# A two-layer hybrid decoder trunk on one core: attention in pairs of heads, one values block for eight heads, the decay table in the queries' place

## The chip, the core and the metric

The kernel runs on one core of one Trainium2 chip. The metric is the device time of one execution in microseconds (us). Three runs of the kernel before gave 844.59, 845.5 and 845.59 us; the median is 845.5 us. The profile comes from a further execution that took 844.61 us, of which the span from the first to the last recorded instruction is 842.8 us.

## The reference, cut to what matters

256 tokens of width 1024 pass two layers, all in float32. A layer normalizes its input, runs three token mixers on it side by side, gates and sums them, projects, adds, and then runs a squared-ReLU MLP:

```python
h = rms_norm(x, attn_norm[l])
o_mla  = mla_branch(...)        # 8 heads, q and k of 96, v of 64, causal softmax
o_moba = moba_branch(...)       # 8 heads of 64, one block of 256: causal softmax
o_ret  = retention_branch(...)  # 4 heads, scores times a decay table, group norm
merged = (sigmoid(g_mla) * (o_mla @ w_branch_mla) + sigmoid(g_moba) * (o_moba @ w_branch_moba)
          + sigmoid(g_ret) * (o_ret @ w_branch_ret))
x = x + merged @ w_out
x = x + squared_relu(rms_norm(x) @ w_up) @ w_down
```

The two attentions each compute, per head, softmax(q k^T) v over 256 tokens.

## The kernel before, in words

**Weights.** TensorE multiplies float32 as products of two rounded parts ("high" and "low"). Every weight block of 128x1024 arrives by a DMA on SyncE's queue into `raw` (line 180), ScalarE copies it to its high part `whi` (line 195), and VectorE subtracts to get the low part `wlo` (line 197). `load_w` (line 167) hands out the block that is wanted and starts `AHEAD` = 1 further one, in the fixed order of `weight_plan`. A product is three matmuls in a row (`three`, lines 216 to 218): high times high, high times low, low times high.

**Program order.** A layer is a list of units (`prog`), each one weight block long: twelve matmuls of 512 columns for the projections. Attention and the like are hung on the units as steps: `at(slot, step)` runs a step right after a unit has been emitted. The units in order are the MLA projections with `mv`, then the gates `gmla0`, `gmla1`, `gmoba0`, `gmoba1` (four units each), then `bmla0`, `bmla1` (the output projection of MLA, two units each), then `rqk`, `rv`, `rg`, `bmoba`, `gret`, `bret`, `wout` and the MLP. The program is built with a scheduler that moves instructions on each engine by its own estimate of when they can start; on the chip each engine then takes them in the order so found. In a `manual_schedule` block the order of the named engine stays as written.

**Attention.** `attention` (line 440) hangs eight heads on units from `first` on. For a head, `scores` (line 407) runs two score matmuls into one of the four PSUM banks of the tag `misc`, VectorE adds the mask and takes the row maxima (lines 413 and 416), scales them (419), ScalarE takes the exponentials with their sums (422), and VectorE divides (425, 427). Two units later `turn` (line 430) transposes the three 128x128 blocks on TensorE (433) into another `misc` bank and ScalarE copies them to `probT` (435). `values` (line 448) multiplies by v for four heads at a time: matmuls that use 64 of the 128 columns of the array, two heads beside each other (460, 462). Its result is split into high and low by `split_plain` (235 on ScalarE, 236 on VectorE): `omlah`, `omlal` for MLA, `omobah`, `omobal` for MoBA. MLA's heads 0 to 3 have their values block at `first + 6`, heads 4 to 7 at `first + 10`, with `first` the unit `mv` 3; MoBA's heads start eight units later, at `gmla1` 3. Before two MoBA heads can be scored, `moba_turn` (line 755) transposes their queries and keys (759) and `stack` (line 379) packs them (389 on ScalarE, 391 to 393 on VectorE).

**Branch.** `branch` (line 485) projects the attention output and multiplies it with its gate `th`. Its unit 0 reads the heads 0 to 3 of `omlah` and `omlal`, its unit 1 the heads 4 to 7. With `between`, given for `bret` alone, half 1 enters a `manual_schedule` of TensorE that `wout_first` leaves.

**Retention.** `ret_scores` (line 797) multiplies its scores with the decay table `DEC`, 6 KB on each partition, loaded once in layer 0 at `gmla1` 0 (line 734). MLA's queries `Q` (8 KB on each partition) are a tile of their own tag.

Of the kernel before, what the change touches and what calls it, by code (L numbers as in the profile page):

```python
# [7 lines left out]
F32 = mybir.dt.float32  # L8
# [5 lines left out]
P = 128  # L14
D = 1024
S = 256
# [100 lines left out]
K_DEC = K_SIN_RT + NT * 32  # L117
K_END = K_DEC + RT_H * 3 * P
# [9 lines left out]
def trunk(ctx: ExitStack, tc: tile.TileContext, gx, wts, consts, gfin, xtok, out):  # L128


    nc = tc.nc
    _, where, _ = weight_plan()

    cp = ctx.enter_context(tc.tile_pool(name="cp", bufs=1))
    wp = ctx.enter_context(tc.tile_pool(name="wp", bufs=1))
    sb = ctx.enter_context(tc.tile_pool(name="sb", bufs=1))
# [5 lines left out]
    X = [GX[:, G_END:].rearrange("p (k s) -> p k s", k=4), cp.tile([P, 4, S], F32, name="x1")]  # L142
    x = gx[:, G_END:].rearrange("p (k s) -> p k s", k=KD)
    K = cp.tile([P, K_DEC], F32, name="K")
    DEC = cp.tile([P, K_END - K_DEC], F32, name="DEC")
    ident = K[:, K_ID : K_ID + P]
    mask = K[:, K_MASK : K_MASK + 2 * P]
    neghalf = cp.tile([P, 8], F32, name="neghalf")
# [17 lines left out]

    def load_w(*key):

        ahead = 0 if key[:2] in ((0, "b0"), (0, "mq"), (0, "b0mq")) else AHEAD
        while order and len(loaded) < ahead + 1:  # L170
            first = order.pop(0)
            loaded[first] = fetch(first)
        return loaded.pop(key)
# [32 lines left out]
    def misc_tile(name="misc"):  # L206
        return ps.tile([P, 512], F32, name=name, tag="misc", bufs=4)
# [18 lines left out]
    def small(name):  # L226
        return sb.tile([P, 8], F32, name=name, tag="st", bufs=12)
# [6 lines left out]
    def split_plain(src, hi, lo):  # L234
        nc.scalar.activation(hi, src, AF.Copy)
        nc.vector.tensor_sub(lo, src, hi.bitcast(F32))
# [165 lines left out]
    def attention_head(score, scale):  # L402


        got = {}

        def scores():
            s_ps = misc_tile("ps_s")
            score(s_ps[:, 0:P], slice(0, P), slice(0, P))
            score(s_ps[:, P : 3 * P], slice(P, S), slice(0, S))  # L410
            p = sb.tile([P, 3 * P], F32, name="prob", bufs=3)
            m = small("smx")
            nc.vector.tensor_tensor_reduce(
                p[:, 0:P], s_ps[:, 0:P], mask[:, P : 2 * P], 1.0, NEG_INF, ALU.add, ALU.max, m[:, 0:1]
            )
            nc.vector.tensor_tensor_reduce(
                p[:, P : 3 * P], s_ps[:, P : 3 * P], mask, 1.0, NEG_INF, ALU.add, ALU.max, m[:, 1:2]
            )
            nc.vector.tensor_scalar(m[:, 2:4], m[:, 0:2], -scale, None, op0=ALU.mult)  # L419
            spans = ((0, P), (P, 3 * P))  # L420
            for i, (a, b) in enumerate(spans):
                nc.scalar.activation(  # L422
                    p[:, a:b], p[:, a:b], AF.Exp, bias=m[:, 2 + i : 3 + i], scale=scale, accum_out=m[:, 4 + i : 5 + i]
                )
            nc.vector.reciprocal(m[:, 6:8], m[:, 4:6])
            for i, (a, b) in enumerate(spans):
                nc.vector.tensor_scalar(p[:, a:b], p[:, a:b], m[:, 6 + i : 7 + i], None, op0=ALU.mult)
            got["p"] = p

        def turn():  # L430
            pt = misc_tile("ps_pt")
            for i, src in enumerate((0, P, 2 * P)):
                nc.tensor.transpose(pt[:, P * i : P * i + P], got["p"][:, src : src + P], ident)  # L433
            pT = sb.tile([P, 3 * P], F32, name="probT", bufs=5)
            nc.scalar.activation(pT, pt[:, : 3 * P], AF.Copy)
            return pT

        return scores, turn

    def attention(oT, score, vs, scale, first):  # L440


        pT = {}

        def turned(h, turn):
            pT[h] = turn()

        def values(h0):


            o, v = misc_tile("po"), vs()
            with tc.manual_schedule(engines={mybir.EngineType.PE}):
                for h in (h0 + 2, h0):
                    cs = slice(S * (h - h0) // 2, S * (h - h0) // 2 + S)
                    for i in range(2):
                        for j in (1, 0):
                            vh = v[i][:, VD * (h + j) : VD * (h + j) + VD]
                            dst = o[64 * j : 64 * j + 64, cs]
                            if i == 0:
                                nc.tensor.matmul(dst, vh, pT[h + j][:, 0:S], start=True, stop=False)  # L460
                            else:
                                nc.tensor.matmul(dst[:, P:S], vh, pT[h + j][:, S : 3 * P], start=False, stop=True)  # L462
            split_plain(o, *(part[:, h0 // 2 : h0 // 2 + 2, :].rearrange("p k s -> p (k s)") for part in oT))

        for h in range(8):
            scores, turn = attention_head(lambda o, qs, ks, h=h: score(h, o, qs, ks), scale)
            at(first + h, scores)
            at(first + h + 2, lambda h=h, turn=turn: turned(h, turn))
            if h % 4 == 3:
                at(first + h + 3, lambda h=h: values(h - 3))  # L470

    def gates(l, key, xn):

# [11 lines left out]
    def branch(l, key, oT, th, merged, between=None):  # L485


        def unit(half, j, accs):
            if j == 0:
                accs.extend(acc_tile() for _ in range(NT))  # L490
            if between and half and j == 0:
                between(0)
            wh, wl = load_w(l, f"{key}{half}", j)
            by_k = [(t, kk) for kk in range(2) for t in range(NT)]
            for t, kk in sorted(by_k) if j else by_k:
                if between and half and j and (t, kk) == (0, 0):
                    between(1)
                if between and half and j and (t, kk) == (1, 0):
                    between(2)
                k, sl = 2 * j + kk, slice(P * t, P * t + P)  # L500
                three(accs[t], oT[0][:, k, sl], oT[1][:, k, sl], wh[:, kk, :], wl[:, kk, :], k == 0, k == 3)
            for t in range(NT) if j else ():
                z = th[half, t]
                if (half, t) in merged:
                    nc.vector.scalar_tensor_tensor(z, z, 1.0, accs[t], op0=ALU.add, op1=ALU.mult)
                    nc.vector.tensor_add(merged[half, t], merged[half, t], z)
                else:
                    merged[half, t] = z
                    nc.vector.scalar_tensor_tensor(z, z, 1.0, accs[t], op0=ALU.add, op1=ALU.mult)

        for half in range(2):
            accs = []
            for j in range(2):
                prog.append(((f"{key}{half}", j), lambda half=half, j=j, accs=accs: unit(half, j, accs)))
# [37 lines left out]
    def at(slot, step):  # L552
        steps.setdefault(slot, []).append(step)

    def slot(key, j):
        return [k for k, _ in prog].index((key, j))
# [9 lines left out]
    def layer(l, xn, before):  # L566

        c0 = []
        c, mla, mqkv, rqkv = {}, {}, {}, {}

        b0 = []
# [71 lines left out]
        else:  # L643
            mq = []
# [85 lines left out]

        omlaT, omobaT, oretT = [], [], []
        th_mla = gates(l, "gmla", xn)
        if l == 0:
            at(slot("gmla1", 0), lambda: tc.keep_in_program_order(nc.sync.dma_start(DEC, consts[:, K_DEC:])))
        first = slot("mv", 3)
        at(first, lambda: omlaT.extend((t4("omlah"), t4("omlal"))))

# [10 lines left out]
        th_moba = gates(l, "gmoba", xn)  # L748
        merged, mT = {}, ([], [])
        branch(l, "bmla", omlaT, th_mla, merged)  # L750
        first = slot("gmla1", 3)
        at(first, lambda: omobaT.extend((t4("omobah"), t4("omobal"))))
        qkT = {}

        def moba_turn(i):
            pt = misc_tile("pqk")
            for a, key in enumerate(("mq", "mk")):
                for t in range(NT):
                    nc.tensor.transpose(
                        pt[:, (2 * a + t) * P : (2 * a + t + 1) * P], mqkv[key][t][:, P * i : P * i + P], ident  # L760
                    )
            qkT[i] = stack(pt)

        for i in range(4):
            at(first + 2 * i - 1, lambda i=i: moba_turn(i))
        attention(
            omobaT,
            lambda h, o, qs, ks: stacked_scores(qkT[h // 2][h % 2], o, qs, ks),
# [16 lines left out]
        rT, or_ps, aT, rg, oret = [], [], {}, [], []  # L785
# [11 lines left out]
        def ret_scores(h):  # L797
            s_ps = misc_tile("ps_r")
            stacked_scores(rT[h], s_ps[:, 0:S], slice(0, S), slice(0, P), swap=True)
            stacked_scores(rT[h], s_ps[:, S : 3 * P], slice(P, S), slice(P, S), swap=True)  # L800
            aT[h] = sb.tile([P, 3 * P], F32, name="retA", tag="prob", bufs=3)
            nc.vector.tensor_mul(aT[h], s_ps[:, : 3 * P], DEC[:, 384 * h : 384 * h + 384])

        def ret_values(h):
            if h == 0:
# [256 lines left out]
        for t in range(NT):  # L1062
# [12 lines left out]
            else:  # L1075

                sl, more = slice(P, 2 * P), misc_tile("plast")
                for half, o in enumerate((accs[3], more)):
                    cs = slice(512 + 256 * half, 768 + 256 * half)
# [24 lines left out]
            if t:  # L1104
                nc.vector.scalar_tensor_tensor(y[:, cs], xr[:, t, cs], r, gf[:, 0, cs], op0=ALU.mult, op1=ALU.mult)
                cs = slice(512, 768)
            else:
                cs = right
# [23 lines left out]
WARM = 7  # L1132
FIRST = 4
WHOLE = 1
AHEAD = 1
T4 = 9


# [75 lines left out]
```

## Time and profile before

| | before |
|---|---|
| runs, us | 844.59, 845.5, 845.59 (median 845.5) |
| the profiled execution, us | 844.61 |
| its span, us | 842.8 |
| granted TensorE clock | 0.999 |
| VectorE busy | 606.1 us, 72% |
| ScalarE busy | 498.7 us, 59% |
| GpSimd busy | 14.4 us, 2% |
| HBM read | 148.22 MB, 177 GB/s over the span |
| share of DMA queue 1 | 56.0% of 16 engines |

The busy time of an engine is the union of its instructions; matmuls overlap each other, so the start of one matmul to the start of the next says what one costs. "PE" is TensorE's matmuls, "PEld" its weight loads, "DVE" VectorE, "ACT" ScalarE, "SP" SyncE. In a row of the timeline stand the start, the length, the engine, the line, the operation, the tiles written and read, the shape and the count of merged instructions; a bracket gives the idle time before it and what ended it.

### The profile page before, as it was taken

To read this page: it belongs to the slowest core of one execution; us is meant where nothing else is said; L and a number is where in the kernel's file an instruction comes from. 1 tells how busy PE (TensorE), PEld (TensorE's weight loads), DVE (VectorE), ACT (ScalarE), POOL (GpSimd) and SP (SyncE) were. 2 spreads that over 40 slices of the span, in tenths; PEclk is the share of its full clock that TensorE was granted. 3 is DMA by queue.
4 is the path that set the end of the run, shared out by engine and by line. 5 is a ranking of instruction groups with operands and counts; after the bars stand their busy time and mean duration, and the time that the engine had idled before them with its cause. 6 is when DMAs were issued, how large, how long until landed. Compare 5 with 4: busy or idle time off the path is not lost.

```text
span 842.8 us, 12495 instructions
## 1 busy us (share of the span) xinstructions
PE 834.7 (99%) x4555; PEld 717.5 (85%) x4555; DVE 606.1 (72%) x1187; ACT 498.7 (59%) x867; POOL 14.4 (2%) x23
## 2 busy tenths in 40 slices
PE   9999999999999999999999999999999999999996
PEld 7888888988998888888888888879889988888886
DVE  7887787787777666666588868867878766556664
ACT  7757766535556555555677667654456555555552
POOL 0000000010000000000000000000100000000000
PEclk9999999999999999999999999999999999999999
DMA  9765444545456656665366545455565565666641
GB/s 355 255 208 183 129 144 153 171 151 183 146 175 222 200 193 185 197 191 182 118 207 220 174 139 164 138 163 155 171 186 161 181 204 184 184 199 184 191 126 51
DMA packets 42397, 150.08 MB, mean 178 GB/s; under 512 B 4704, under 2 KB 5088, under 8 KB 42336
## 3 DMA queue, kind: packets, MB, share of 16 engines
q1 hardware_dynamic: 41760, 148.42, 56.0%
q8 instruction: 36, 0.59, 0.3%
q10 hardware_dynamic: 576, 0.87, 0.3%
q14 instruction: 25, 0.20, 0.1%
HBM read 148.22 MB, written 1.05 MB: 177 GB/s over the span
## 4 chain that ended last, share of the span: by engine, by line
PE 98%; issue 1%; DMA 0%; DVE 0%; ACT 0%; POOLq 0%; POOL 0%; DVEq 0%
PE acc L216 20%; PE acc L217 20%; PE acc L218 20%; PE pup L955 13%; PE pup L957 7%; PE acc L906 5%; PE ps_pt L433 1%; PE ps_s L739 1%; PE po L460 1%; PE ps_s L400 1%; PE acc L632 0%; PE acc L635 0%; PE acc L633 0%; PE po L462 0%; PE pmt L878 0%
## 5 line engine op out<-in xcount | busy, mean ns | idle before, releaser
L197 DVE TENSOR_TENSOR wlo<-raw,whi 128x1024 fp32r<-128x1024 f32 (+3 forms) x286 | 336.9, 1184 | 164.2 <-ACT whi L195 100.7
L195 ACT ACTIVATE whi<-raw 128x1024 fp32r<-128x1024 f32 (+3 forms) x286 | 292.4, 1026 | 197.4 <-PE acc L218 92.5
L216 PE MATMUL acc<-whi,xs 128*128 128x512 f32 (+1 forms) x352 | 139.5, 398 | 0.0
L217 PE MATMUL acc<-wlo,xs 128*128 128x512 f32 (+1 forms) x352 | 138.5, 393 | 0.0
L218 PE MATMUL acc<-whi,xs 128*128 128x512 f32 (+1 forms) x352 | 138.3, 394 | 0.0
L955 PE MATMUL pup<-xs,whi 128*128 128x512 f32 x496 | 121.5, 391 | 0.0
L955 PEld LDWEIGHTS pup<-xs,whi 128*128 128x128 f32 x496 | 92.2, 188 | 18.6
L216 PE MATMUL acc<-whi,sq 128*128 128x512 f32 (+1 forms) x256 | 99.8, 390 | 0.0
L217 PE MATMUL acc<-wlo,sq 128*128 128x512 f32 (+1 forms) x256 | 99.6, 389 | 0.0
L218 PE MATMUL acc<-whi,sq 128*128 128x512 f32 (+1 forms) x256 | 98.4, 388 | 0.0
L218 PEld LDWEIGHTS acc<-whi,xs 128*128 128x128 f32 x352 | 66.2, 188 | 12.9 <-issue 0.2
L216 PEld LDWEIGHTS acc<-whi,xs 128*128 128x128 f32 x352 | 66.1, 188 | 12.7 <-issue 0.2
L217 PEld LDWEIGHTS acc<-wlo,xs 128*128 128x128 f32 x352 | 66.3, 188 | 12.0 <-issue 0.2
L957 PE MATMUL pup<-xs,wlo 128*128 128x256 f32 x496 | 68.5, 283 | 0.0
L957 PEld LDWEIGHTS pup<-xs,wlo 128*128 128x128 f32 x496 | 65.8, 191 | 2.9
L966 ACT ACTIVATE relu<-relu 128x256 f32<-128x256 f32 x64 | 25.8, 409 | 55.1 <-DVE relu L965 55.1
L218 PEld LDWEIGHTS acc<-whi,sq 128*128 128x128 f32 x256 | 48.0, 188 | 9.9
L216 PEld LDWEIGHTS acc<-whi,sq 128*128 128x128 f32 x256 | 48.2, 188 | 9.1
L217 PEld LDWEIGHTS acc<-wlo,sq 128*128 128x128 f32 x256 | 48.2, 188 | 8.8
L422 ACT ACTIVATE prob<-prob,smx 128x128 f32<-128x128 f32 x64 | 28.4, 445 | 11.5 <-DVE smx L419 11.1
L906 PE MATMUL acc<-mTh,whi 128*128 128x256 f32 x128 | 32.0, 286 | 0.0
L906 PE MATMUL acc<-mTh,wlo 128*128 128x256 f32 x128 | 31.7, 283 | 0.0
(276 smaller groups left out, 1192.8 us busy)
## 6 DMA issues: line engine op xcount, KB each, us to landing
raw<-wts SPq DMA_DIRECT2D x264, 512.0 KB, 3.9
raw<-wts SPq DMA_DIRECT2D x7, 464.0 KB, 7.2
raw<-wts SPq DMA_DIRECT2D x4, 416.0 KB, 3.3
xrow<-xtok SPq DMA_DIRECT2D x4, 256.0 KB, 8.3
raw<-wts SPq DMA_DIRECT2D x3, 256.0 KB, 4.0
DEC<-consts SPq DMA_DIRECT2D x1, 768.0 KB, 7.1
x<-gx SPq DMA_DIRECT2D x1, 512.0 KB, 6.4
gf<-gfin SPq DMA_DIRECT2D x1, 512.0 KB, 4.4
```

Source lines behind the costliest of these rows:

```text
L195: nc.scalar.activation(hi[:, cs], raw[:, cs], AF.Copy)
L197: nc.vector.tensor_sub(lo[:, cs], raw[:, cs], hi[:, cs].bitcast(F32))
L216: nc.tensor.matmul(o, ah, bh, start=start, stop=False)
L217: nc.tensor.matmul(o, ah, bl, start=False, stop=False)
L218: nc.tensor.matmul(o, al, bh, start=False, stop=stop)
L400: nc.tensor.matmul(o, b if swap else a, a if swap else b, start=i == 0, stop=i == 1)
L422: nc.scalar.activation(p[:, a:b], p[:, a:b], AF.Exp, bias=m[:, 2 + i : 3 + i], scale=scale, accum_out=m[:, 4 + i : 5 + i])
L433: nc.tensor.transpose(pt[:, P * i : P * i + P], got["p"][:, src : src + P], ident)
L906: nc.tensor.matmul(acc[:, :S], a, b, start=i == 0 and ks[0] == 0, stop=i == len(jobs) - 1 and ks[-1] == KD - 1)
L955: nc.tensor.matmul(u, w, xm.both(k), start=k == 0, stop=False)
L957: nc.tensor.matmul(u[:, 0:S], w, xm.k(k)[0], start=False, stop=k == KD - 1)
L966: nc.scalar.activation(s, s, AF.Square)
```

## The change

- `attention` takes the heads in pairs: two units hold the transposes of one pair (the later head first) and the scores of the next pair, in place of one head at each unit.
- `values` runs once for all eight heads, into two PSUM banks, at `first + 11`; in each pair the order of the two heads is turned round. The bank of the heads 4 to 7 is written and split first, that of the heads 0 to 3 last.
- `turn` writes its three transposes in reverse; `probT` has 9 buffers (5 before), `prob` 4 (3 before).
- The decay table is no constant any more: it is loaded in each layer at `gmoba1` 0 into the place of `Q`.
- `bret`'s fixed TensorE order starts with half 0 in place of half 1.
- `moba_turn` runs one unit earlier.
- `load_w` goes two blocks ahead for `gret1`, `bret0`, `bret1` and `wout`, one ahead elsewhere.

```diff
-    DEC = cp.tile([P, K_END - K_DEC], F32, name="DEC")
...
-        ahead = 0 if key[:2] in ((0, "b0"), (0, "mq"), (0, "b0mq")) else AHEAD
+        ahead = 0 if key[:2] in ((0, "b0"), (0, "mq"), (0, "b0mq")) else 2 if key[1] in LATE else 1
...
-            p = sb.tile([P, 3 * P], F32, name="prob", bufs=3)
+            p = sb.tile([P, 3 * P], F32, name="prob", bufs=4)
...
-            for i, src in enumerate((0, P, 2 * P)):
+
+            for i, src in reversed(list(enumerate((0, P, 2 * P)))):
                 nc.tensor.transpose(pt[:, P * i : P * i + P], got["p"][:, src : src + P], ident)
-            pT = sb.tile([P, 3 * P], F32, name="probT", bufs=5)
+            pT = sb.tile([P, 3 * P], F32, name="probT", bufs=9)
...
-        def values(h0):
-
-
-            o, v = misc_tile("po"), vs()
+        def values():
+
+
+            o, v = [misc_tile("po") for _ in range(2)], vs()
             with tc.manual_schedule(engines={mybir.EngineType.PE}):
-                for h in (h0 + 2, h0):
-                    cs = slice(S * (h - h0) // 2, S * (h - h0) // 2 + S)
+                for h in (6, 4, 2, 0):
+                    cs = slice(S * (h % 4) // 2, S * (h % 4) // 2 + S)
                     for i in range(2):
-                        for j in (1, 0):
+                        for j in range(2):
                             vh = v[i][:, VD * (h + j) : VD * (h + j) + VD]
-                            dst = o[64 * j : 64 * j + 64, cs]
+                            dst = o[1 - h // 4][64 * j : 64 * j + 64, cs]
...
-            split_plain(o, *(part[:, h0 // 2 : h0 // 2 + 2, :].rearrange("p k s -> p (k s)") for part in oT))
-
-        for h in range(8):
-            scores, turn = attention_head(lambda o, qs, ks, h=h: score(h, o, qs, ks), scale)
-            at(first + h, scores)
-            at(first + h + 2, lambda h=h, turn=turn: turned(h, turn))
-            if h % 4 == 3:
-                at(first + h + 3, lambda h=h: values(h - 3))
+            for i in (1, 0):
+                split_plain(o[1 - i], *(part[:, 2 * i : 2 * i + 2, :].rearrange("p k s -> p (k s)") for part in oT))
+
+
+        heads = [attention_head(lambda o, qs, ks, h=h: score(h, o, qs, ks), scale) for h in range(8)]
+        for i in range(5):
+            slot_i = first + 2 * i
+            for h in (2 * i - 1, 2 * i - 2) if 1 <= i <= 4 else ():
+                at(slot_i, lambda h=h: turned(h, heads[h][1]))
+            for h in (2 * i, 2 * i + 1) if i < 4 else ():
+                at(slot_i, heads[h][0])
+        at(first + 11, values)
...
-            if between and half and j == 0:
+            if between and (half, j) == (0, 0):
                 between(0)
...
-        if l == 0:
-            at(slot("gmla1", 0), lambda: tc.keep_in_program_order(nc.sync.dma_start(DEC, consts[:, K_DEC:])))
+
+        def load_decay():
+
+            mla["decay"] = sb.tile([P, K_END - K_DEC], F32, name="DEC", tag="Q", bufs=1)
+            tc.keep_in_program_order(nc.sync.dma_start(mla["decay"], consts[:, K_DEC:]))
+
...
+        at(slot("gmoba1", 0), load_decay)
...
-            at(first + 2 * i - 1, lambda i=i: moba_turn(i))
+            at(first + 2 * i - 2, lambda i=i: moba_turn(i))
...
-            aT[h] = sb.tile([P, 3 * P], F32, name="retA", tag="prob", bufs=3)
-            nc.vector.tensor_mul(aT[h], s_ps[:, : 3 * P], DEC[:, 384 * h : 384 * h + 384])
+            aT[h] = sb.tile([P, 3 * P], F32, name="retA", tag="prob", bufs=4)
+            nc.vector.tensor_mul(aT[h], s_ps[:, : 3 * P], mla["decay"][:, 384 * h : 384 * h + 384])
...
-AHEAD = 1
+
+LATE = ("gret1", "bret0", "bret1", "wout")
```

## The prediction

> **What bounds the kernel now.** I read the page first: its busy shares, and the chain that ended last. Then I asked the waits of TensorE alone.
>
> ```profile
> span 842.8 us, 12495 instructions
> PE 834.7 (99%) x4555; PEld 717.5 (85%) x4555; DVE 606.1 (72%) x1187; ACT 498.7 (59%) x867; POOL 14.4 (2%) x23
> PE 98%; issue 1%; DMA 0%; DVE 0%; ACT 0%; POOLq 0%; POOL 0%; DVEq 0%
> ```
> ```profile
> PE warm L548 <- DVE zero L155: 1.4, 1, 1.4
> ```
>
> TensorE is busy for 99% of the span, it makes up 98% of the chain, and its list of waits has one row, at the very start. So no matmul waits for VectorE, ScalarE or a DMA; all of them run under it. The time is the sum of the steps from matmul to matmul. A change can gain only by making that sum shorter, and it loses whatever wait it puts into it. The span is 842.8 us of an execution of 844.6 us; 1.8 us lie around it and stay.
>
> The changed program holds the same 4,429 matmuls, counted in the built order of each engine. Only their order differs, and so two questions remain: what the new order saves at its seams, and whether it brings a matmul too close behind what feeds it.
>
> **The seams: a gain of about 1.5 us.** The timeline of TensorE around MLA's second values block of layer 0:
>
> ```profile
> 102.40 0.39 PE L217 MATMUL acc<-wlo,xs 128*128 128x512 f32 x1
> 102.62 0.39 PE L218 MATMUL acc<-whi,xs 128*128 128x512 f32 x1
> 102.94 0.65 PE L460 MATMUL po<-probT,vml 128*64 128x256 f32 x4
> 103.43 0.39 PE L462 MATMUL po<-probT,vml 128*64 128x128 f32 x4
> 103.64 0.60 PE L460 MATMUL po<-probT,vml 128*64 128x256 f32 x4
> 104.08 0.39 PE L462 MATMUL po<-probT,vml 128*64 128x128 f32 x4
> 104.39 0.50 PE L216 MATMUL acc<-whi,xs 128*128 128x512 f32 x1
> 104.73 0.39 PE L217 MATMUL acc<-wlo,xs 128*128 128x512 f32 x1
> ...
> 114.77 0.39 PE L216 MATMUL acc<-whi,omlah 128*128 128x512 f32 x1
> ```
>
> Read the starts. A plain matmul of 512 columns steps 0.22 to 0.23. The one ahead of the block steps 0.32, 0.09 more. Inside, a pair of heads costs 0.21 + 0.44 = 0.65, two pairs 1.30, but the block takes 1.45: 0.15 more. The matmul behind it steps 0.34, 0.11 more. That is 0.35 for going into and out of half-width matmuls. Before, there are eight such blocks (two attentions, two halves, two layers); after, four of sixteen instead of eight instructions each: 4 x 0.35 = 1.4 us saved. Turning round j within a pair changes nothing that a row shows.
>
> ```profile
> 97.96 0.49 PE L433 MATMUL ps_pt<-K,prob 128*128 128x128 f32 x3
> 98.29 0.38 PE L759 MATMUL pqk<-K,mq 128*128 128x128 f32 x2
> 98.51 0.38 PE L759 MATMUL pqk<-K,mk 128*128 128x128 f32 x2
> 98.64 0.48 PE L218 MATMUL acc<-whi,xs 128*128 128x512 f32 x1
> 98.96 0.39 PE L216 MATMUL acc<-whi,xs 128*128 128x512 f32 x1
> ...
> 99.65 0.22 PE L400 MATMUL ps_s<-stk 128*128 128x128 f32 x1
> ...
> 100.11 0.39 PE L216 MATMUL acc<-whi,xs 128*128 128x512 f32 x1
> ```
>
> A transpose steps 0.11 (three in 0.33). Leaving transposes for projections takes 0.09 off one step (0.13 for 0.22) and puts 0.09 on the next (0.32): almost nothing. Pairing the heads cuts such runs from 97 to 74; at 0 to 0.02 each that is 0 to 0.5, and I take 0.1. A MoBA head's four score matmuls take 0.46.
>
> **The new distance between the MLA values and `bmla0`.** In the rows above, MLA's last values end at 104.39 and the first matmul that reads `omlah` starts at 114.77: over 10 us of other work for the copies. In the changed order, layer 0 reads as follows (h is the MoBA head; each line runs in its engine's order):
>
> ```
> PE:  scores h0, h1 | 4 pqk | 16 of gmoba1 (its last) | transposes h1, h0 | scores h2, h3
>      | values MLA 4-7 | values MLA 0-3 | 4 pqk | bmla0 on omlah of heads 0-3
> DVE: max h0, max h1, scale both, stk, divide h0, divide h1, wlo, stk, max h2, wlo, scale h2,
>      max h3, scale h3, divide h2, omlal 4-7, divide h3, omlal 0-3
> ACT: exp h0, exp h1, whi, stk, th, th, whi, probT h1, probT h0, exp h2, omlah 4-7, exp h3, omlah 0-3
> ```
>
> The values stand behind MoBA's heads 0 to 3 because all of them take turns on four `misc` banks, and between their end and `bmla0` there are only four transposes: 0.44 us. The other gate matmuls are used up by then, and `rqk`'s need the PSUM banks that `bmla0` and `bmla1` hold. So TensorE now stands at the end of a chain through VectorE and ScalarE. Its prices come from a stretch in which both work without a break:
>
> ```profile
> 112.42 0.27 DVE L413 CUSTOM_DVE_ANT_0 prob<-ps_s,K 128x128 f32<-128x128 f32 x1
> 113.08 0.17 DVE L419 TENSOR_SCALAR smx<-smx 128x2 f32<-128x2 f32 x1
> 113.33 1.23 DVE L197 TENSOR_TENSOR wlo<-raw,whi 128x1024 fp32r<-128x1024 f32 x1
> 114.59 0.43 DVE L391 TENSOR_TENSOR stk<-pqk,stk 64x256 fp32r<-64x256 f32 x1
> 115.69 0.17 DVE L425 RECIPROCAL smx<-smx 128x2 f32<-128x2 f32 x1
> 115.89 0.55 DVE L427 TENSOR_SCALAR prob<-prob,smx 128x128 f32<-128x128 f32 x2
> ```
> ```profile
> 113.33 0.58 ACT L389 CAST stk<-pqk 64x512 fp32r<-64x512 f32 x1
> 113.93 0.40 ACT L422 ACTIVATE prob<-prob,smx 128x128 f32<-128x128 f32 x1
> 114.95 1.27 ACT L479 ACTIVATE th<-acc,half 128x512 f32<-128x512 f32 x2
> 116.10 1.06 ACT L195 ACTIVATE whi<-raw 128x1024 fp32r<-128x1024 f32 x1
> 117.05 0.49 ACT L435 ACTIVATE probT<-ps_pt 128x384 f32<-128x384 f32 x1
> 117.42 0.58 ACT L389 CAST stk<-pqk 64x512 fp32r<-64x512 f32 x1
> ```
> ```profile
> 85.43 0.60 ACT L235 ACTIVATE omlah<-po 128x512 fp32r<-128x512 f32 x1 [0.51 <-PE po L462]
> ```
>
> From start to start: max 0.66, scale 0.2, wlo 1.26, the three `stk` operations 1.1, divide 0.75; on ScalarE `stk` 0.6, exp 1.0, two `th` 1.15, whi 0.95, probT 0.4, `omlah` 0.6. The time is counted from the end of h1's scores.
>
> - VectorE starts max h0 at 0.2 and ends both at 1.55, the scales at 2.0, `stk` at 3.1. ScalarE's exps end at 2.8 and 3.8. Divide h0 ends at 3.85, divide h1 at 4.6. TensorE's cover is 0.44 + 16 x 0.227 = 4.07, so the transposes wait **0.6**, to 4.65.
> - They end at 5.3, scores h2 at 5.75. Scores h3 need a bank that the next `stk` on VectorE frees: whi (ends 4.75), wlo behind it (6.0), `stk` (7.1). Lost: **1.4**, to 7.15.
> - Values 4-7 need the bank of h2's scores, free after max h2 at 7.8. Scores h3 end at 7.6: **0.25** lost. The values then run from 7.85 to 10.6, the `pqk` to 11.05.
> - ScalarE's probT h0 rewrites a buffer that the first pair of values reads, so it runs at 8.7 to 9.1. Behind it exp h2 waits for its scale, which stands behind the second wlo (9.25), and ends at 10.25; `omlah` 4-7 ends at 10.8, exp h3 at 11.8, `omlah` 0-3 at 12.4. `bmla0` starts at 12.45: **1.4** lost.
>
> Layer 0 loses 3.65 us. In layer 1 the two first scores stand 1.5 us apart, and the cover is 28 matmuls; the same walk gives 0.85 (divide h1 stands behind a wlo and a `stk`), 0.5 (values behind max h2) and 1.65 (`omlah` 0-3 behind both exps): 3.0. Together **6.65 us**. The bounds: what remains if all but the last link runs early is 0.6 for the copy plus 0.05 less 0.44 per layer, 0.4 in all; if every step costs its whole length rather than the step to the next (exp with its reads 1.27 for 1.0, and so on), the walk gives about 10.
>
> **The other edits, at nothing.**
>
> ```profile
> DEC<-consts SPq DMA_DIRECT2D x1, 768.0 KB, 7.1
> ```
> ```profile
> 203.34 0.68 DVE L236 TENSOR_TENSOR oretl<-oy,oreth 128x512 fp32r<-128x512 f32 x1
> 205.68 0.69 DVE L236 TENSOR_TENSOR oretl<-oy,oreth 128x512 fp32r<-128x512 f32 x1
> ```
> ```profile
> 205.84 0.39 PE L216 MATMUL acc<-whi,oreth 128*128 128x512 f32 x1
> ```
>
> The decay load is issued once more, and now waits on SyncE's queue for the last MLA score, with the weight loads behind it. That score precedes it by some 3 us in the new order, so it should be past; the next weight block is cast over 10 us later, and the landing of 7.1 us fits. Uncovered, it would cost up to 7.1 a layer. The table is read at `rg`, sixteen units on. `bret` in written order reads `oretl` at 205.84 + 2 x 0.23 = 206.3 (ready at 204.0) and for its second unit near 209.0 (ready at 206.4): over 2 us of slack. `LATE` fetches earlier where nothing waits; four `raw` buffers limit it. The extra `prob` and `probT` buffers only lift waits. MoBA's values have 12 units of `rqk`, `rv` and `rg` ahead of `bmoba`, so the merged block costs nothing there.
>
> **The sum.** 844.6 - 1.5 + 6.65 = 849.75 on the profiled execution. The median lies 0.9 above it: 845.5 + 5.15, about **850.5 us**.
>
> **The rivals.**
>
> - *The chain ends in time* (the other side). VectorE and ScalarE idle 28% and 41% of the span; if they enter this stretch ahead, with whi and wlo done before the maxima, divide h1 ends before 4.07 and both exps before the values do. It decides at a loss of 1.5 us in all: below that the seams win. With the 0.4 that must remain: 845.5 - 1.5 + 0.4 = 844.4, at best 844.0 with none.
> - *The chain is short but there.* Half of the walk, 3.3 us: 847.3.
> - *The clock drops in the gaps.* Cold matmuls of the same width show at the start:
>
> ```profile
> 1.43 3.29 PE L548 MATMUL warm<-zero 128*128 128x512 f32 x7 [1.43 <-DVE zero L155]
> ```
>
> Seven in 3.29 us, 0.47 each for 0.23: a loss of about 1.7 us for each cold start. One a layer on top of the walk gives 854, two 857.5. Against it: no single wait above is over 1.65 us, with matmuls between them. By the Trainium skill, "TensorE: Matmul & The Clock Gate", section "Part 1: The HAM clock gate", the clock halves after one idle window of about 3.4 us; by that rule this case doesn't come about. No run here shows a gap of such a length yet.
>
> - *The change doesn't save at its seams*: the cost sits in each bank's block of eight, not in the way in and out. The rows speak against it (0.65 + 0.65 with no seam inside). It would add 1.4: 852, within the forecast's range.
>
> **Chances.** The forecast with a walk of 4.5 to 10: 0.60, 848.5 to 854. Short chain: 0.20, 846 to 848.5. In time: 0.10, 844 to 845.5. Cold clock or a longer chain: 0.10, up to 858. The range 845.0 to 855.5 leaves out about 0.08 on each side. 0.2% is 1.7 us, about what a measurement of this kernel can tell from no change. Faster (under 843.8): 0.05. Same (to 847.2): 0.15. Slower: 0.80.
>
> **What would show it.** In the profile after, TensorE's waits should have rows they lack now: `ps_pt` (433) on VectorE's divide, `ps_s` on `stk`, `po` on the maxima, and largest `acc` of `bmla0` on ScalarE's `omlah`, twice 1.4 or more, near 115 and 525 us, and nothing else. `po` should show four blocks and the projection steps 0.23 behind the waits; 0.43 there would be the cold clock. If the waits sum to under 2 us, my walk is wrong at VectorE's entry; if a wait stands on whi or a DMA, it is the decay load that I priced at nothing.

## The result, and the profile after

The changed kernel takes 848.03 us (median of 7 runs, 847.66 to 848.63); the kernel before took 845.29 us beside it (median of 7, 844.59 to 845.59). The ratio is 1.0037, with a 95% interval of 1.0027 to 1.0047: 2.7 us slower. The profiled execution took 848.03 us as well. Its page:

```profile
span 846.2 us, 12483 instructions
...
PE 834.5 (99%) x4555; PEld 719.5 (85%) x4555; DVE 606.2 (72%) x1187; ACT 496.5 (59%) x867; POOL 14.3 (2%) x23
...
PE 95%; DVE 1%; ACT 1%; issue 1%; DMA 0%; POOLq 0%; POOL 0%; DVEq 0%; ACTq 0%
```

TensorE is busy for as long as before (834.5 for 834.7 us, with 4555 matmuls in both profiles; the prediction's count of 4,429 stands in neither), and the span has grown by 3.4 us. VectorE and ScalarE, at 0% of the chain before, now hold 1% each. So it is not the work that got longer; TensorE waits. Its list of waits says for whom (engine, tile, line, releaser: us in total, times, longest; idle times shorter than about 0.15 us are not in it):

```profile
PE acc L215 <- ACT omlah L234: 1.8, 2, 1.0
PE warm L552 <- DVE zero L154: 1.4, 1, 1.4
PE ps_s L399 <- DVE low L392: 1.2, 1, 1.2
PE po L460 <- DVE smx L415: 0.3, 1, 0.3
PE ps_pt L433 <- DVE prob L426: 0.2, 1, 0.2
```

The row of `warm` was there before. The other four are new and hold 3.5 us. The busy times by stretch of the span place them (PE, PEld, DVE, ACT and POOL each with its count, then the granted clock):

```profile
98.00:128.00 30.00, 27.87 (x168) 22.88 (x167) 25.43 (x77) 20.52 (x47) 0.00 (x0) 1.00 0.35 111
508.00:538.00 30.00, 28.44 (x170) 23.30 (x170) 24.65 (x71) 22.36 (x49) 0.00 (x0) 1.00 0.56 183
128.00:160.00 32.00, 32.00 (x182) 26.55 (x181) 24.45 (x50) 19.36 (x33) 0.00 (x0) 1.00 0.51 166
538.00:575.00 37.00, 37.00 (x200) 30.41 (x199) 29.02 (x65) 21.28 (x40) 0.00 (x0) 1.00 0.48 143
```

TensorE is short of 2.13 us in 30 around MLA's values of layer 0 and of 1.56 around those of layer 1, and of nothing beside them. The granted clock reads 1.00 in both.

Now the places themselves, TensorE's timeline in layer 0:

```profile
110.00 0.39 PE L217 MATMUL acc<-whi,xs 128*128 128x512 f32 x1
110.49 0.84 PE L433 MATMUL ps_pt<-K,prob 128*128 128x128 f32 x6
...
111.52 0.28 PE L399 MATMUL ps_s<-low,stk 128*128 128x256 f32 x1
113.02 0.30 PE L399 MATMUL ps_s<-stk 128*128 128x128 f32 x1 [1.22 <-DVE low L392]
...
113.43 0.28 PE L399 MATMUL ps_s<-low,stk 128*128 128x256 f32 x1
113.64 0.65 PE L460 MATMUL po<-probT,vml 128*64 128x256 f32 x4
...
116.67 0.38 PE L768 MATMUL pqk<-K,mk 128*128 128x128 f32 x2
117.86 0.50 PE L215 MATMUL acc<-whi,omlah 128*128 128x512 f32 x1 [0.81 <-ACT omlah L234]
118.19 0.40 PE L216 MATMUL acc<-wlo,omlah 128*128 128x512 f32 x1
118.43 0.39 PE L215 MATMUL acc<-whi,omlah 128*128 128x512 f32 x1
```

and in layer 1:

```profile
527.46 0.39 PE L217 MATMUL acc<-whi,xs 128*128 128x512 f32 x1
528.10 0.88 PE L433 MATMUL ps_pt<-K,prob 128*128 128x128 f32 x6 [0.25 <-DVE prob L426]
...
529.62 0.28 PE L399 MATMUL ps_s<-low,stk 128*128 128x256 f32 x1
530.17 0.65 PE L460 MATMUL po<-probT,vml 128*64 128x256 f32 x4 [0.28 <-DVE smx L415]
...
533.20 0.38 PE L768 MATMUL pqk<-K,mk 128*128 128x128 f32 x2
534.61 0.50 PE L215 MATMUL acc<-whi,omlah 128*128 128x512 f32 x1 [1.03 <-ACT omlah L234]
```

Idle time in brackets is less than what a wait costs, because matmuls overlap; the starts tell the whole. A transpose run begins 0.49 after the plain matmul ahead of it in layer 0 and 0.64 in layer 1, for a step of 0.23: 0.26 and 0.41 lost. (In layer 0 this leaves only 0.10 of idle time, too little for a row in the list.) Scores h3 begin 1.50 after the last score of h2 for a step of 0.12: 1.38 lost (none in layer 1). The values begin 0.21 and 0.55 after the last score; 0.21 is what the way into half-width matmuls costs by itself (0.12 and 0.09), so 0 and 0.34 are lost. `bmla0` begins 1.19 and 1.41 after the row of the last two `pqk`, where such a step took 0.13 before (98.51 to 98.64): 1.06 and 1.28 lost. Layer 0 loses 2.7, layer 1 2.0, together **4.7 us**. The span grew by 3.4; the 1.3 between them is what the four blocks of values fewer saved (four runs of values in place of eight).

### The profile page after: what moved, and what is told of

It is laid out like the page before. It is cut to its first block, busy times and chain, and to the rows that moved or that the text cites. A ratio compares the mean times of both kernels' runs of the same rounds, so it can differ in the third digit from the quotient of the medians.

```text
span 846.2 us, 12483 instructions
## 1 busy us (share of the span) xinstructions
PE 834.5 (99%) x4555; PEld 719.5 (85%) x4555; DVE 606.2 (72%) x1187; ACT 496.5 (59%) x867; POOL 14.3 (2%) x23
## 3 DMA queue, kind: packets, MB, share of 16 engines
HBM read 149.01 MB, written 1.05 MB: 177 GB/s over the span
## 4 chain that ended last, share of the span: by engine, by line
PE 95%; DVE 1%; ACT 1%; issue 1%; DMA 0%; POOLq 0%; POOL 0%; DVEq 0%; ACTq 0%
PE acc L215 20%; PE acc L216 19%; PE acc L217 19%; PE pup L964 13%; PE pup L966 7%; PE acc L915 5%; PE ps_s L747 1%; PE ps_pt L433 1%; PE ps_s L399 1%; ACT prob L421 1%; PE po L460 1%; PE acc L637 0%; PE acc L636 0%; PE acc L639 0%; PE b L636 0%
```

## The experiments

All were timed against the kernel before, whose median beside them was 844.8 to 845.2 us (845.29 beside the kernel after), so medians of different rounds compare to about 0.5 us. Two theories stood against each other at the start: the place of MLA's one values block, too close ahead of `bmla0` and behind MoBA's first scores, is the cause; or it is something else in the change (the pairing, the decay load, the order of `bret`).

**Values in two blocks again, heads still in pairs** (e1):

```diff
-        def values():
+        def values(h0):
...
-                for h in (6, 4, 2, 0):
+                for h in (h0 + 2, h0):
...
-            for i in (1, 0):
+            for i in (h0 // 4,):
...
-        at(first + 11, values)
+        at(first + 6, lambda: values(0))
+        at(first + 10, lambda: values(4))
```

> The kernel after, but with the values of each attention in two blocks of four heads again: heads 0 to 3 at first + 6, heads 4 to 7 at first + 10; the heads stay in pairs, the decay table and all else as after. Theory (the distance between the values and bmla0 costs; the seams gain): the five waits of TensorE near 110 to 118 and 528 to 535 us go, up to a rest of 0.5 us, and the 1.4 us of the seams come back, so about 845.3 us, 2.5 to 3 us under the kernel after and level with the kernel before. Rival 1 (pairing the heads is what brings the waits, not the merged block): the waits on the divide, on stk and on the maxima stay, 1 to 1.5 us a layer, about 847.5. Rival 2 (the decay load or the fixed order of bret is the cost): no change from after, 848.

Measured: 844.91 us, ratio 1.0001 (0.9992 to 1.0010). Its list of waits:

```profile
PE warm L553 <- DVE zero L154: 1.4, 1, 1.4
```

All four new rows are gone, with the pairs kept. The pairing isn't the cause, and neither is anything else that e1 keeps (the decay load, the order of `bret`, `LATE`, the buffers, the earlier `moba_turn`); with eight runs of values the time is that of the kernel before.

**Heads 0 to 3 first** (e2), since `bmla0`'s first unit reads these:

```diff
-                for h in (6, 4, 2, 0):
+                for h in (2, 0, 6, 4):
...
-            for i in (1, 0):
+            for i in (0, 1):
```

> The kernel after, but the values block computes and splits the heads 0 to 3 first, which bmla0's first unit reads, and the heads 4 to 7 last. Theory: omlah of the heads 0 to 3 no longer stands behind exp h3 and behind the other half's copy, and TensorE has the 1.3 us of the other half's values and the 0.44 us of the pqk as cover; the wait of acc on omlah (1.05 us in layer 0, about 1.3 in layer 1) falls under 0.6 in each, the waits on the divide, stk and smx stay: about 846.4 us, 1.2 to 2.0 under the kernel after. Rival (both copies stand behind exp h2, which comes late because of the second wlo): the wait falls only by the 0.6 us of one copy in each layer, 847.0 us. Rival 2 (the second unit of bmla0 now waits for the heads 4 to 7): it takes back half of the gain, 847.

Measured: 846.45 us, 1.0018 (1.0009 to 1.0027). Its list of waits, below the row of `warm`:

```profile
PE ps_s L399 <- DVE low L392: 1.2, 1, 1.2
PE po L460 <- DVE smx L415: 0.3, 1, 0.3
PE ps_pt L433 <- DVE prob L426: 0.2, 1, 0.2
```

The wait on `omlah` is gone, and the other three stand as they were. 1.6 us come back of the 2.3 that this wait costs; the trace holds six runs of values here in place of four, because MoBA's block fell into two in each layer, and two seams at 0.35 are the other 0.7.

**The one block two units earlier** (e3):

```diff
-        at(first + 11, values)
+        at(first + 9, values)
```

> The kernel after, but with the one values block of eight heads at first + 9 in place of first + 11, in both attentions: the MLA values stand right behind MoBA's first two scores and ahead of its first transposes, with the matmuls of gmoba1 between them and bmla0. Theory: the merged block is not slow by itself, it only stands too late; with 16 or more matmuls of 0.23 us (3.7 us) behind it, omlah is ready in time, and the transposes and scores of MoBA have the 2.6 us of the values as cover. All waits under 0.5 us in each layer, the seams' 1.4 us kept: 843.9 us, 1.4 under the kernel before and 4 under the kernel after. Rival 1 (the chain through stk and the exps stays the bound and shifts to MoBA's own scores): waits of 1 to 2 us in each layer, 846. Rival 2 (the cost is not in these waits): 848, as after.

Measured: 844.35 us, 0.9994 (0.9985 to 1.0002). The one wait beside `warm`, and the timeline ahead of `bmla0` in layer 0:

```profile
PE acc L217 <- DVE oretl L235: 0.3, 2, 0.2
```
```profile
109.57 0.38 PE L768 MATMUL pqk<-K,mk 128*128 128x128 f32 x2
113.45 0.49 PE L433 MATMUL ps_pt<-K,prob 128*128 128x128 f32 x3
113.70 0.48 PE L215 MATMUL acc<-whi,omlah 128*128 128x512 f32 x1
```

Between the `pqk` behind the values and `bmla0` there are now 4 us of other matmuls, and no wait at all is left in this stretch. So one block of eight heads isn't slow; its place was. It misses the expected 843.9 by 0.45, and a row that neither the kernel before nor the one after has says where: `bret`, the projection of the retention, waits for `oretl`, the low part of the retention's output. The same timeline there:

```profile
201.95 0.60 PE L849 MATMUL pot<-K,oret 128*128 128x128 f32 x4
205.60 0.39 PE L215 MATMUL acc<-whi,oreth 128*128 128x512 f32 x1
205.82 0.39 PE L216 MATMUL acc<-wlo,oreth 128*128 128x512 f32 x1
206.36 0.50 PE L217 MATMUL acc<-whi,oretl 128*128 128x512 f32 x1 [0.15 <-DVE oretl L235]
```

MoBA's heads and the retention behind them come later in this order. The last four transposes of `pot`, which feed `oretl`, stand in one run 3.65 us ahead of `bret` (201.95 to 205.60); in the kernel after they stand in two runs, 5.7 and 4.3 us ahead (202.38 and 203.76 to 208.07). The row says 0.15 of idle time for each layer, but the starts say more: from `bret`'s first product to the first of the MLP, e3 takes 36.18 us in each layer, the kernels before and after 35.70. So this wait costs 0.48 a layer. e1 has it in layer 1 alone, with idle time just under what the list takes in (36.14 us there, 35.70 in layer 0).

**The decay table alone** (e4: the kernel before with the table loaded per layer into the queries' place) and **the order of `bret` with `LATE` alone** (e5: the kernel before with `(half, j) == (0, 0)` and the look-ahead of 2):

> The kernel before with one edit of the change alone: the decay table is loaded in each layer at gmoba1 0 into the place of the queries. Theory (priced at nothing in the prediction): as before within 0.3 us, 845.3 us, no row for a wait of TensorE beyond the one at the start. Rival (the load holds the weight DMAs behind it on SyncE's queue, or comes into the gate matmuls late): up to 2 us more, 846 to 847.5, with a wait on whi or wlo near 110 or 527 us.

> The kernel before with two edits of the change alone: bret's fixed TensorE order starts with half 0, and LATE lets load_w go two blocks ahead for gret1, bret0, bret1 and wout. Theory (both priced at nothing in the prediction): as before within 0.3 us, 845.0 us. Rival (the fixed order takes away room that the scheduler used: in the run with the values at first + 9 bret waited twice 0.15 us on oretl and its stretch was 0.6 us a layer longer in steps): 0.3 to 1.2 us above before, with a row of acc on oretl.

Measured: 844.81 us, 0.9999 (0.9991 to 1.0008), and 844.98 us, 1.0000 (0.9991 to 1.0008). Neither has a wait beside `warm`. In the kernel after, the two loads land in 5.8 us:

```profile
DEC<-consts SPq DMA_DIRECT2D x2, 768.0 KB, 5.8
```

By themselves, the load and the two edits at `bret` are worth nothing that could be told here: the intervals leave room for some 0.8 us each way.

**The block at first + 9 with `bret`'s old order** (e6), to win back what `oretl` cost:

```diff
-            if between and (half, j) == (0, 0):
+            if between and half and j == 0:
```

> The run with the values at first + 9, with bret's fixed order starting with half 1 again, as in the kernel before. Theory: the two waits of acc on oretl go and the 0.6 us a layer that the stretch behind 200 and 615 us had gained over before go with them, because the free order puts eight products of oreth ahead of the first oretl: 843.2 us, 1.1 below the run with the values at first + 9 and 1.8 below the kernel before. Rival (only the waits of 0.15 us count): 844.0. Rival 2 (the fixed order of half 0 matters in no way): 844.35 as that run.

Measured: 845.99 us, 1.0010 (1.0001 to 1.0018): 1.64 us worse in place of 1.1 better. The waits on `oretl` went, but:

```profile
PE pmt L887 <- DVE th L510: 0.8, 2, 0.4
```
```profile
215.61 0.40 PE L217 MATMUL acc<-whi,oretl 128*128 128x512 f32 x1
216.43 0.66 PE L887 MATMUL pmt<-K,th 128*128 128x128 f32 x4 [0.41 <-DVE th L510]
```

With the free order, `bret`'s first half ends later: VectorE's product with the gate (509), which needs that half, starts 7.0 us behind `bret`'s first product, and 5.7 us in e3 (212.50 less 205.50, 211.28 less 205.60). Its merge (510) is late in turn, and the transposes `pmt` ahead of `wout` wait for it. From `bret`'s first product to the MLP a layer takes 36.9 us for e3's 36.18; over both layers that is 1.45 of the 1.64. My expectation fell: the order by half 0 is what keeps a late retention cheap.

**MLA's block alone at first + 9** (e7: MoBA's stays at `first + 11`), and **that with `bret`'s old order** (e8):

> The kernel after, but with MLA's values alone at first + 9; MoBA's values stay at first + 11. Theory (the whole loss sits at MLA's values, none at MoBA's): the five waits go as they did with both at first + 9, so 844.4 us or less; MoBA's place decides at most 0.3 us. Rival (MoBA's merged block also waits or holds something up at first + 11): 845 to 846.

> The kernel after, but with MLA's values alone at first + 9 and with bret's fixed order starting with half 1 again. Theory: 843.2 us, as with both values at first + 9 and that order, and as much below its neighbour without the bret edit as bret's stretch costs there (0 if the retention steps fall as in the kernel after, where bret waited for nothing, up to 1.2 if as with both at first + 9). Rival: MoBA's place at first + 11 costs 0.5 or more, 843.7 to 844.5.

Measured: 844.32 us, 0.9993 (0.9984 to 1.0002), and 845.89 us, 1.0011 (1.0002 to 1.0020). They tell less than was meant: the scheduler puts MoBA's block at the same place from either slot, and all 4555 matmuls stand in the order of e3 and of e6. They serve as repeats: 844.32 for 844.35, 845.89 for 845.99. That MLA's slot alone is the edit in e3 follows all the same.

**The kernel after with `bret`'s old order** (e9, the same edit as in e6):

> The kernel after, with bret's fixed order starting with half 1 as in the kernel before, all else as after. The order of bret was worth nothing alone in the kernel before (0.0) and 1.6 us with the values at first + 9, where the four retention transposes stand in one run and oretl is ready only as bret starts. In the kernel after the transposes stand in two runs, as before. Theory (the order of bret pays only where retention is late): 848.0 us, as after within 0.3, no wait of pmt. Rival (it pays wherever heads are paired): 849.5 with two waits of pmt on th.

Measured: 847.72 us, 1.0035 (1.0022 to 1.0047), waits as in the kernel after, none on `th`. So that order pays 1.6 us where retention comes late, and nothing where it doesn't.

**MoBA's heads two units earlier**, on top of e3: with heads 4 to 7 first (e10), with heads 0 to 3 first (e11), and with heads 4 to 7 first in layer 1 alone (e12):

```diff
-        first = slot("gmla1", 3)
+        first = slot("gmla1", 1)              # e10, e11
+        first = slot("gmla1", 1 if l else 3)  # e12
```

> The run with the values at first + 9 (heads 4 to 7 first), with MoBA's heads two units earlier, at gmla1 1 in place of gmla1 3. The built order then has retention 40 matmul rows earlier, its transposes in two runs as in the kernel before, but only four pqk and three transposes between MLA's values and bmla0 (0.44 and 0.33 us). Theory (the cover behind the values decides): the oretl waits go (1.1 us less in steps), and an acc wait on omlah of 0.5 to 1.3 us a layer comes back in layer 0, so 844.0 to 845.5. Rival (the exps of MoBA are what makes omlah late; here they have been done before): no wait, 843.2.

> As the run with MoBA's heads two units earlier, with the heads 0 to 3 of the values computed and split first. The built order parts MoBA's values into two runs of eight in layer 0, and both values blocks of layer 1 by a matmul or more: two or three seams of 0.35 come back. Theory: no wait at omlah (1.3 us of values and 0.44 of pqk as cover) and none at oretl: 843.2 + 0.35 x 3, about 844.0. Rival: MoBA's first scores, now in the stretch of MLA's last pair, make another wait of 0.5 or more: 844.7 or over.

> The run with the values at first + 9, with MoBA's heads two units earlier in layer 1 alone (gmla1 1 there, gmla1 3 in layer 0). Layer 1 showed no wait in either place, and with the earlier heads its retention stretch cost 0.46 us in steps for 1.07. Theory: the wait of acc on oretl in layer 1 goes, nothing comes back: 843.75 us, 0.6 under the run with the values at first + 9 in both, 1.2 under the kernel before. Rival (the two stretches do not add up, something else in layer 1 takes it back): 844.3.

Measured: e10 844.48 us, 0.9996 (0.9987 to 1.0005); e11 845.47 us, 1.0007 (0.9998 to 1.0016); **e12 843.79 us, 0.9985 (0.9976 to 0.9994)**. The new rows in the lists of waits, first e10, then e11 (e12 has the row of `warm` alone):

```profile
PE ps_pt L433 <- DVE prob L426: 0.9, 1, 0.9
```
```profile
PE acc L215 <- ACT omlah L234: 0.5, 1, 0.5
```

And e10 at that place:

```profile
114.84 0.38 PE L768 MATMUL pqk<-K,mk 128*128 128x128 f32 x2
116.15 0.52 PE L433 MATMUL ps_pt<-K,prob 128*128 128x128 f32 x3 [0.93 <-DVE prob L426]
116.42 0.47 PE L215 MATMUL acc<-whi,omlah 128*128 128x512 f32 x1
```

In e10 the waits on `oretl` are gone, as the built order promised, and a wait of 0.93 stands again in layer 0, in the stretch where one was expected but on another releaser: the transposes, in front of `bmla0` now, wait for a divide, and the four `pqk` between them and the values are too little cover. In e11 `omlah` waited 0.5 us in spite of the changed halves, against the theory. My 844.0 was too low by 1.5: its own sum, 843.2 + 3 x 0.35, is 844.25, and `bmla0` begins 0.91 after the row of the last `pqk` for a step of 0.13 (115.35 to 116.26), 0.8 more. Where the remaining 0.4 is I did not settle. e12 takes the earlier heads only where they cost no wait. Its list is clear, but that isn't the whole of it: `bret` of layer 0 still takes 36.17 us, with the idle time ahead of `oretl` just under what the list takes in; layer 1 is back at 35.70. Of the change and the twelve runs it is the one whose interval lies below 1, if narrowly, and it came out where it was expected (843.75): 1.4 us under the kernel before that ran beside it (845.22), 1.0 to 1.2 under its median in the other rounds of experiments, and some 4 under the kernel after.

## Why the prediction was right, and where a size was off

- **The seams, -1.5.** Held: 4.7 us of lost steps and a span 3.4 longer leave 1.3. e1 and e3 agree: three runs of values more are 1.05 at 0.35 each, e3 pays 0.96 at `bret` where e1 pays 0.44, and the difference of the two, 0.53, compares with 0.56 measured (844.91 and 844.35, of one round, with a noise of about that size).
- **The chain behind the values, +6.65.** The mechanism was right and its size too big: 4.7. Six of its seven links showed, in the order given; five stand in the list of waits with the releasers named, the sixth (the first, 0.26) is too short for a row. Term by term, predicted and measured: layer 0, transposes 0.6 and 0.26; scores h3 on `stk` 1.4 and 1.38; values behind max h2 0.25 and 0; `bmla0` 1.4 and 1.06; layer 1, 0.85 and 0.41; 0.5 and 0.34; 1.65 and 1.28. Undoing the place alone (e3) removed every one of them.

Why the predicted terms are too large shows in the two engines' timelines of layer 0. VectorE:

```profile
106.32 0.29 DVE L412 CUSTOM_DVE_ANT_0 prob<-ps_s,K 128x128 f32<-128x128 f32 x1
...
109.80 0.55 DVE L426 TENSOR_SCALAR prob<-prob,smx 128x128 f32<-128x128 f32 x2
110.54 1.22 DVE L196 TENSOR_TENSOR wlo<-raw,whi 128x1024 fp32r<-128x1024 f32 x1 [0.20 <-ACT whi L194]
...
112.90 0.29 DVE L412 CUSTOM_DVE_ANT_0 prob<-ps_s,K 128x128 f32<-128x128 f32 x1
```

and ScalarE:

```profile
107.69 0.40 ACT L421 ACTIVATE prob<-prob,smx 128x128 f32<-128x128 f32 x1 [0.29 <-DVE smx L418]
...
108.59 0.39 ACT L421 ACTIVATE prob<-prob,smx 128x128 f32<-128x128 f32 x1
...
114.99 0.39 ACT L421 ACTIVATE prob<-prob,smx 128x128 f32<-128x128 f32 x1
...
115.87 0.58 ACT L234 ACTIVATE omlah<-po 128x512 fp32r<-128x512 f32 x1
...
117.22 0.58 ACT L234 ACTIVATE omlah<-po 128x512 fp32r<-128x512 f32 x1
```

The scores of h1 end at 106.12, the walk's zero. VectorE enters at 0.20, as the walk had it. But ScalarE's first exp starts at 1.6 for 1.8, because maxima and scales took a little less (a head's maxima 0.56 from start to start, 106.32 to 106.88, for 0.66), and a head's exps take 0.90 from start to start (107.69 to 108.59) where the walk had 1.0: divide h1 ends at 110.35, that is 4.2 for 4.6. Max h2 starts at 6.8 for 7.1, exp h2 at 8.9 for 9.25, and from its start to the end of the last `omlah` it is 2.8 (114.99 to 117.80) for 3.15. No wait stood on another engine than the one named; steps a little shorter than their prices made 0.7 by the end of layer 0, where `bmla0` starts at 11.74 for 12.45. Layer 0 lost 0.95 less than walked (2.70 for 3.65). The other 0.25 is on TensorE's side: its own matmuls in this stretch took 9.04 us (11.74 less 2.70) where the walk has 8.80, and so covered more. The prediction gives layer 1's walk by its results only, and its 1.0 us isn't traced to steps here.

- **The other edits, at nothing.** Right for this kernel, within the noise, by e1, e4, e5 and e9. That `bret`'s order is worth 1.6 us beside another order of retention (e6, e8) was outside the walk.
- **The sum.** 844.6 - 1.5 + 4.7 = 847.8 on a profiled execution; measured 848.03. The term that was mis-sized is the walk, by 2 us. A second, smaller one is the 0.9 us that the prediction put between a profiled execution and the median: after, both are 848.03. Sign and range held (848.03 lies in 845.0 to 855.5), but the forecast case's own range, 848.5 to 854, didn't: the time fell into the case called short but there, priced at half the walk, to which I gave 0.20. The measured walk of 4.7 does lie in the 4.5 to 10 of the forecast case, at its low end; without the 0.9 that case would have started at 847.6.
- **The rivals.** The chain didn't end in time: that needed a loss under 1.5 us. The change does save at its seams, as said above. The clock didn't drop: behind both waits of `bmla0` the first step is 0.33 or 0.34 (0.32 behind transposes in the kernel before, without a wait: 98.64 to 98.96) and the next ones are 0.23 to 0.24 (118.19, 118.43), not the 0.47 of the kernel's first matmuls. (The granted clock can't tell: it reads 1.00 over the first 3 us of the kernel before as well, where the steps are that long.) The longest gap behind the start was 1.22 us. By the Trainium skill, "TensorE: Matmul & The Clock Gate", section "Part 1: The HAM clock gate", the clock is halved after an idle window of about 3.4 us. The trace agrees as far as it goes, since no gap of that length occurred.

## What to carry to other kernels

Merging small blocks on a saturated engine saves what the rows of the seams say, but the merged block has one place, and both its ends count: what it now stands behind, and how much other work is left before its first reader. Walk the helper engines' queues from the last scores to that reader; where a wait comes out, the answer may be to move the block two units (844.35 us here) rather than to split it again (844.91), both from 848.03. A list of waits shows where TensorE stands, and the starts show what that costs: 0.15 us of idle time was 0.48 us at `bret`. And a fixed order can be worth nothing in one schedule and 1.6 us in the next, so an edit tried alone says little about the same edit beside others.

## What the runs showed that was not expected

Moving one step by two units shifted the scheduler's whole order behind it: in e3 the retention's first values stand 55 matmuls later than in the kernel after, in both layers, and a new wait appeared at `bret`, 100 us behind the moved values of layer 0 (106.5 to 206.4). A slot may also decide nothing: with MLA's values at `first + 9`, MoBA's at `first + 9` and at `first + 11` gave the same order on TensorE.
